# Key tiles of latent and context tokens by 512-column products in one layer of a diffusion backbone

## The chip, the core and the metric

One NeuronCore of a Trainium2 chip runs the whole layer. It has a matrix engine (TensorE, PE in the profile), three engines for elementwise work (VectorE or DVE, ScalarE or ACT, GpSimd or POOL), queues that issue DMA transfers (SyncE's, SP, does most of that), an on-chip memory of 128 partitions (SBUF) and banks in which products accumulate (PSUM, 512 float32 columns a bank and partition). Each engine works through its own queue in order; semaphores hold an instruction back until others are done. The metric is the device time of one execution in microseconds.

## The reference

The layer takes 256 latent tokens `x` and 256 context tokens `ctx`, both 2048 wide, in float32. Cut to what matters here:

```python
h_l = modulate(rms_norm(x, norm1_w), sh1, sc1)          # (1, 256, 2048)
h_c = modulate(rms_norm(ctx, norm1_w), sh1c, sc1c)      # (1, 256, 2048)
gq_l, gk_l, gv_l, gr_l, gaf_l, gab_l, dq_l, dk_l, dv_l = split(h_l @ w_in)
gq_c, gk_c, gv_c, gr_c, gaf_c, gab_c, dq_c, dk_c, dv_c = split(h_c @ w_in)
# gated linear attention, 8 heads of 64/128, forward and backward over chunks of 64 tokens,
#   over the context first, then over the latent tokens
# differential attention, 8 heads: two softmaxes over 512 keys [k_c, k_l], a = p1 - lam * p2
g_a, g_b = split(sigmoid(h_l @ w_gate + b_gate))
x = x + g1 * ((g_a * (gla @ w_proj_gla) + g_b * (diff @ w_proj_diff)) @ w_out)
x = x + g2 * conv_ffn(modulate(rms_norm(x, norm2_w), sh2, sc2))    # width 5632, convolution of 3
```

Only the latent stream is returned. The context needs keys (`gk`, `dk`), values (`gv`, `dv`) and decays, while queries, gates and all that follows are of the latent tokens alone.

## The kernel before

**Products of split halves.** Every float32 operand is split into a high part (rounded to TensorE's fp32r format) and a low part, the difference. A product is then three: high by high, high by low, low by high. ScalarE makes the high half of a weight tile (L211, `whi`), VectorE the low half (L218, `wlo`; in the feed-forward part GpSimd takes some), and the halves of the activations are kept for the whole layer: `A[k]` (tile name `a`) for the latent and `B[k]` (`c`) for the context, for each of 16 K tiles of 128 rows a tile `[128, 2, 256]` with the low half in front and the high half behind it. The lists `H` hold the halves of both.

**Two ways to multiply.** `col_tile` (L243) makes a 128-column piece of a projection of the latent tokens alone, with the output's columns as rows: high weights by both halves of `A[k]` in one product of 512 columns, low weights by the high half, 256 columns. Where latent and context tokens are both wanted, `both_tile` (L334) makes three products of 256 columns for each stream, six a K tile, into the two halves of one bank. `col_tile2` (L760) runs it over 16 K tiles for two key tiles of the GLA heads (`gk`) and seven of the differential heads (`dk`). Values (`gvb`, `dvb`) are made the other way round, activations as the weights and 512 weight columns streaming (`value_rows`, L288).

**The stages.** First the sweep (up to about 132 us): while the modulation weights stream in, each K tile of `x` and `ctx` is normed and modulated (`stage`, L528) and at once multiplied with part of `w_in`: four row groups (`sweep_row`) and three key tiles (`sweep_col`, L562, six products of 256 columns for each), with modulation products (`ab`) for the next K tile between them. Everything in the sweep has a fixed order. Then the GLA stage (to about 450 us), the differential attention with the gate tiles (to about 760), the merge, and the feed-forward part.

**What sets the order.** Outside the sweep a scheduler orders each engine's queue before the run, with a timeline of its own and priorities. In the GLA stage the four head pairs (`gla_pair`, L788) have a high priority, and projections fill in between: `gvb`, `gq`, `gk`, `dk`, `gr`, then the first value chunk `dvb` of the differential heads and the first queries `dq`. A pair is a long serial chain: decay logits `z` on PE, logarithms and scans on ACT and DVE to `rc` (L826), transposed on PE (`kT`, L831), copied, multiplied to `state` (L837), and then scores `sc` (L863) in rounds: first two plain ones, then seven levels of a halving scheme, two levels a round. For a level, POOL makes four differences of the running decay sums (L890 to L893), ACT their exponential (L894), DVE the product with queries and keys (L895), PE the scores, DVE the masked copy (L908). There are two buffers `e` for it, so that a round starts when the scores of the round before have read theirs. At the end come `o` (L914, L917), its sum of squares `oss` (L681) and the norm. The pairs use the same buffers one after another.

The differential stage needs the memory of the GLA stage, so it begins when the fourth pair is done: the first value chunk stands in four accumulator banks until then, and the first query projection `dq` takes one of two banks that `oss` uses as well (`aux_bank`, L1018). In `dv_chunk` (L994) the second chunk takes the K tiles in the order 12 to 15, then 0 to 11, so that context halves of the last tiles come free early: the halves of the keys (`ks`, in `halves`, L1025) are put in their place, later the gates (`C`), one for each `c` tile. Dot products of further modulation weights (`ada_next`, L703: a load into one of two buffers `araw`, and a VectorE product L363) are strewn over all of this, one or half of one for each tile.

Of the kernel before, what the change touches and what calls it, by code (L numbers as in the profile page):

```python
# [9 lines left out]
F32 = mybir.dt.float32  # L10
F32R = mybir.dt.float32r
# [7 lines left out]
P = 128  # L19
D = 2048  # L20
T = 256
KT = D // P
# [129 lines left out]
def layer_kernel(tc, I, out):  # L152
    nc = tc.nc
    V, S, G, PE = nc.vector, nc.scalar, nc.gpsimd, nc.tensor
    es = ExitStack()
    with es:
        cp = es.enter_context(tc.tile_pool(name="const", bufs=1))
        st = es.enter_context(tc.tile_pool(name="stream", bufs=1))
        hp = es.enter_context(tc.tile_pool(name="acts", bufs=1))
# [165 lines left out]

        A, B, C = [], [], []
        (hl, ll), (hc, lc) = H = ([], []), ([], [])
        def spare(k, j, name):  # L330

            return hp.tile([P, 512], F32, tag=f"{'ac'[j]}{k}", name=name)

        def both_tile(b, k, whi, wlo, sl, first, last):  # L334

            for j, (hi, lo) in enumerate(H):
                o = b[:, j * T:(j + 1) * T]
                PE.matmul(o, whi[:, sl], hi[k], start=first and j == 0, stop=False)
                PE.matmul(o, whi[:, sl], lo[k], start=False, stop=False)  # L339
                i = PE.matmul(o, wlo[:, sl], hi[k], start=False, stop=last and j == 1)  # L340
            return i


        cb = cp.tile([P, D], F32, name="cb")
# [25 lines left out]
        with tc.tile_pool(name="first", bufs=1) as p1:  # L370
            kept = tc.keep_in_program_order

            def pinned(*args, **kw):

                return kept(PE.matmul(*args, **kw))  # L375
# [21 lines left out]
            dots_of, at = [], 0  # L397
# [129 lines left out]

            def stage(k, m, streams=(0, 1), lows=()):  # L528

                for s in streams:  # L530
                    Y, n, (hi, lo) = (A, B)[s], "ac"[s], H[s]
                    Y.append(hp.tile([P, 2, T], F32R, tag=f"{n}{k}", name=f"{n}{k}"))
                    hi.append(Y[k][:, 1, :])
                    lo.append(Y[k][:, 0, :])
                for s in streams:
                    x = x_tile(s, k)
                    kept(V.scalar_tensor_tensor(x, x, m[:, 1, s:s + 1], z1[:, s * T:(s + 1) * T],
                                                op0=ALU.mult, op1=ALU.mult))
# [20 lines left out]
                pinned(o, hi[k][:, ts], w[1][:, :n], start=False, stop=False)  # L559
                pinned(o, lo[k][:, ts], w[0][:, :n], start=False, stop=k == KT - 1)  # L560

            def sweep_col(k, w, g, streams=(0, 1)):  # L562
                sl = slice(g * P, (g + 1) * P)
                for s in streams:
                    hi, lo = H[s]
                    o = sweep[4 + g][:, s * T:(s + 1) * T]
                    pinned(o, w[0][:, sl], hi[k], start=k == 0 and s == 0, stop=False)
                    pinned(o, w[1][:, sl], hi[k], start=False, stop=False)
                    pinned(o, w[0][:, sl], lo[k], start=False, stop=k == KT - 1 and s == 1)


            pin[0] = True
# [6 lines left out]
            for s in range(2):  # L579
                o = ss[:, s * T:(s + 1) * T]  # L580
# [401 lines left out]
        with tc.tile_pool(name="diff", bufs=1) as pd:  # L982
# [11 lines left out]
            def dv_chunk(j):  # L994
                banks = [acc_bank("dvb") for _ in range(4)]

                def emptied(t):
                    (V.tensor_copy if t % 2 else S.copy)(dv[:, t, 512 * j:512 * (j + 1)], banks[t])


                turn = [6, 7, 0, 1, 2, 3, 4, 5] if j else list(range(8))
                for q in turn:
                    if q in turn[1:3]:
                        flush((later, latest)[turn.index(q) - 1])
                    raw = fetch(I["w_dv"][j, q].rearrange("p a b -> p (a b)"), 1024)
                    ws = []
                    for a in range(2):
                        def halves_of(a=a):
                            if j or q > 1:
                                ada_next(0.5 if j else 1)  # L1010
                            return split(raw[:, a * 512:(a + 1) * 512], 512)
                        ws.append((2 * q + a, halves_of))
                    value_rows(banks, ws, 512, 2 * turn[0], 2 * turn[-1] + 1, emptied)

            def dq_tile(h):
                ada_next(0.5)
# [8 lines left out]
            def halves(h):  # L1025

                qs[h] = pd.tile([P, 2, T], F32R, tag="qs", bufs=2, name="qs")
                split_act(qs[h][:, 0, :], qs[h][:, 1, :], dq[h])
                ks[h] = [hp.tile([P, 512], F32R, tag=f"c{KT - 4 + 2 * (h % 2) + j}", name="ks") for j in range(2)]
                split_act(*ks[h], dk[h])  # L1030

            pms, pTs = {}, {}
# [49 lines left out]
            def gate_tile(j):  # L1082
                ada_next(GATE_ADA[len(gates)])
                b = acc_bank("gate")
                col_tile(I["w_gate"][j], A, b)
                if j == len(C):
                    C.append(hp.tile([P, 2, T], F32, tag=f"c{j}", name=f"C{j}"))
                gates[j] = C[j % KT][:, j // KT, :]
                S.activation(gates[j], b[:, :T], AF.Identity, bias=vcol("b_gate", j))
                V.tensor_tensor(gates[j], b[:, T:], gates[j], op=ALU.add)  # L1090
# [159 lines left out]
        with tc.tile_pool(name="ffn", bufs=1) as pf:  # L1250
# [65 lines left out]

            def turn(m):

                rows.append([hp.tile([P, 512], F32, tag=f"a{4 * t + m}", name="row") for t in range(2)])
                turned = st.tile([P, 1024], F32, tag="araw", bufs=2, name="turned").rearrange("p (c t) -> p c t", c=4)  # L1320
                for c in range(4):
                    V.transpose(turned[:, c, :], x1[4 * m + c])  # L1322
                for p in range(4):
                    for q in range(8):
                        to = rows[m][q // 4].rearrange("p (c n) -> p c n", c=4)
                        nc.gpsimd.dma_start(to[32 * (q % 4):32 * (q % 4 + 1), :, 32 * p:32 * (p + 1)],  # L1326
                                            turned[32 * p:32 * (p + 1), :, 32 * q:32 * (q + 1)])
# [31 lines left out]
            def done(h, t, n, cols=slice(0, 512)):  # L1359

                o = slice(1024 * h + 512 * n + cols.start, 1024 * h + 512 * n + cols.stop)
                y = hp.tile([P, 512], F32, tag=f"a{8 + (4 * h + 2 * t + n + (cols.start > 0)) % 8}", name="y")[:, :cols.stop - cols.start]
                V.tensor_tensor(y, banks[h][t][n][:, cols], cb[:, o], op=ALU.mult)
                V.tensor_tensor(y, y, rows[2 * h + n][t][:, cols], op=ALU.add)
                nc.scalar.dma_start(out[t * P:(t + 1) * P, o], y)
# [35 lines left out]
```

## Time and profile before

| | |
|---|---|
| median of 3 runs | 1680.33 us (1679.37 to 1680.52) |
| profiled execution | 1679.91 us, its span in the trace 1677.6 us |
| PE busy | 1664.8 us, 10052 products |
| DVE, ACT, POOL busy | 1303.0, 978.6, 340.0 us |
| DMA | 370.82 MB, 221 GB/s over the span |
| first 120 us | DMA at 356 to 408 GB/s, its 16 engines full |

The page's second part cuts the span in 40 slices and shows the busy tenths of each engine; the chain is followed back from the last instruction, at each step to what released it. A row of a timeline gives start, length, engine, line, operation and tiles; lengths of matmuls overlap, so the price of a product is the distance from one start to the next in an unbroken run.

### The profile page before, as it was taken

Reading aid. Unit: us, or ns where it says so; the run is one execution under the profiler, and the core shown is the slowest. Engines: PE = TensorE matmul, PEld = TensorE weight load, DVE = VectorE, ACT = ScalarE, POOL = GpSimd, SP = SyncE. Lnnn points to the kernel's source line nnn. Section 1 sums busy time; section 2 is a strip of 40 time slices with the busy share of each in tenths; the row PEclk is TensorE's granted clock in tenths of the full one; section 3 lists DMA queues with packets and bytes.
Section 4 is the critical chain, followed back from the end, with each engine's and each line's share of the span. In section 5 each row is a group of like instructions: output and inputs, shape, how many; then the busy total and the mean of one; then the engine's idle time right before and its main releaser. Section 6 shows DMA issues by size and latency. Waiting matters only on the chain.

```text
span 1677.6 us, 28522 instructions
## 1 busy us (share of the span) xinstructions
PE 1664.8 (99%) x10052; PEld 1439.8 (86%) x10052; DVE 1303.0 (78%) x2479; ACT 978.6 (58%) x1977; POOL 340.0 (20%) x440
## 2 busy tenths in 40 slices
PE   9999999999999999999999999999999999999998
PEld 7779999998788888888888998888888888888887
DVE  5887877768687988788988897888888787755655
ACT  5335465755356777656766686666666666544443
POOL 0001313232210000001223200222222222684000
PEclk9999999999999999999999999999999999999999
DMA  9996744336564655688887566767777676676664
GB/s 383 408 355 215 227 139 154 126 113 206 171 205 147 187 190 189 205 292 273 272 270 247 178 202 212 237 222 240 239 236 237 223 238 213 211 217 209 216 195 142
DMA packets 110831, 370.82 MB, mean 221 GB/s; under 512 B 14432, under 2 KB 19552, under 8 KB 110688
## 3 DMA queue, kind: packets, MB, share of 16 engines
q1 hardware_dynamic: 102112, 362.51, 64.8%
q10 hardware_dynamic: 4032, 4.37, 0.8%
q0 software_dynamic: 4544, 2.14, 0.6%
q8 instruction: 78, 1.28, 0.3%
q14 instruction: 65, 0.53, 0.1%
HBM read 364.73 MB, written 2.10 MB: 219 GB/s over the span
## 4 chain that ended last, share of the span: by engine, by line
PE 95%; DMA 2%; DVE 2%; ACT 1%; issue 0%; DVEq 0%; SPq 0%; ACTq 0%
PE down L1353 14%; PE upg L269 9%; PE upv L269 9%; PE gate L269 7%; PE upv L271 5%; PE upg L271 5%; PE sweep L375 5%; PE gate L271 4%; PE mix L269 4%; PE mix L271 2%; PE pgb L269 2%; PE pga L269 2%; PE dk L340 2%; PE dvb L286 2%; PE dk L339 2%; PE dvb L285 2%
## 5 line engine op out<-in xcount | busy, mean ns | idle before, releaser
L211 ACT CAST whi<-wraw 128x512 fp32r<-128x512 f32 (+2 forms) x1004 | 605.5, 608 | 392.4 <-DVE wlo L218 111.3
L218 DVE TENSOR_TENSOR wlo<-wraw,whi 128x512 fp32r<-128x512 f32 (+2 forms) x932 | 635.6, 690 | 225.9 <-ACT whi L211 214.0
L269 PE MATMUL upg<-a,whi 128*128 128x512 f32 x656 | 229.0, 391 | 0.0
L269 PE MATMUL upv<-a,whi 128*128 128x512 f32 x656 | 229.0, 391 | 0.0
L1353 PE MATMUL down<-whi,g 128*128 128x512 f32 x704 | 216.6, 389 | 0.0
L271 PE MATMUL upv<-a,wlo 128*128 128x256 f32 x656 | 182.8, 280 | 0.0
L271 PE MATMUL upg<-a,wlo 128*128 128x256 f32 x656 | 182.6, 280 | 0.0
L269 PE MATMUL gate<-a,whi 128*128 128x512 f32 x512 | 179.8, 397 | 0.0
L218 POOL TENSOR_TENSOR wlo<-wraw,whi 128x512 fp32r<-128x512 f32 x72 | 100.5, 1395 | 387.9 <-ACT whi L211 370.7
L363 DVE CUSTOM_DVE_ANT_0 araw<-araw,cb 128x1024 f32<-128x1024 f32 x128 | 162.3, 1270 | 15.5 <-DMA araw<-in_w_ada 15.5
L1353 PEld LDWEIGHTS down<-whi,g 128*128 128x128 f32 x704 | 132.1, 188 | 27.3
L269 PEld LDWEIGHTS upv<-a,whi 128*128 128x128 f32 x656 | 122.4, 187 | 26.6
L269 PEld LDWEIGHTS upg<-a,whi 128*128 128x128 f32 x656 | 122.4, 187 | 26.6
L271 PE MATMUL gate<-a,wlo 128*128 128x256 f32 x512 | 139.9, 283 | 0.0
L1353 PE MATMUL down<-wlo,g 128*128 128x512 f32 x352 | 136.9, 389 | 0.0
L271 PEld LDWEIGHTS upv<-a,wlo 128*128 128x128 f32 x656 | 123.9, 189 | 0.5
L271 PEld LDWEIGHTS upg<-a,wlo 128*128 128x128 f32 x656 | 123.9, 189 | 0.5
L269 PEld LDWEIGHTS gate<-a,whi 128*128 128x128 f32 x512 | 94.3, 188 | 19.6 <-issue 0.7
L271 PEld LDWEIGHTS gate<-a,wlo 128*128 128x128 f32 x512 | 96.4, 188 | 5.7 <-issue 1.8
L269 PE MATMUL mix<-a,whi 128*128 128x512 f32 x256 | 88.8, 396 | 0.0
L1353 PEld LDWEIGHTS down<-wlo,g 128*128 128x128 f32 x352 | 66.1, 188 | 13.8
L1326 POOL DMA_DIRECT2D row<-turned x128 | 69.4, 551 | 26.0 <-DVE turned L1322 17.6
(360 smaller groups left out, 3432.7 us busy)
## 6 DMA issues: line engine op xcount, KB each, us to landing
wraw<-in_w_up SPq DMA_DIRECT2D x164, 512.0 KB, 4.4
araw<-in_w_ada SPq DMA_DIRECT2D x128, 512.0 KB, 5.0
wraw<-in_w_down SPq DMA_DIRECT2D x88, 512.0 KB, 4.3
wraw<-in_w_gate SPq DMA_DIRECT2D x64, 512.0 KB, 4.2
wraw<-in_w_in SPq DMA_DIRECT2D x58, 512.0 KB, 4.3
ada<-in_w_ad SPq DMA_DIRECT2D x52, 512.0 KB, 10.0
wraw<-in_w_proj SPq DMA_DIRECT2D x32, 512.0 KB, 4.7
wraw<-in_w_out SPq DMA_DIRECT2D x32, 512.0 KB, 4.7
```

The source lines that it names most:

```text
L211: copied[0] = S.copy(hi[:, :n], raw)
L218: i = e.tensor_tensor(lo[:, :n], raw, hi[:, :n].bitcast(F32), op=ALU.subtract)
L269: i = PE.matmul(b.rearrange("p (a b) -> p a b", a=2), whi[:, sl], acts[k], start=first, stop=last)
L271: i = PE.matmul(b[:, T:], wlo[:, sl], acts[k][:, 1, :], start=False, stop=last)
L285: PE.matmul(o, lo[k][:, ts], whi[:, sl], start=False, stop=False)
L286: return PE.matmul(o, hi[k][:, ts], wlo[:, sl], start=False, stop=last)
L339: PE.matmul(o, whi[:, sl], lo[k], start=False, stop=False)
L340: i = PE.matmul(o, wlo[:, sl], hi[k], start=False, stop=last and j == 1)
L363: i = V.tensor_tensor_reduce(raw, raw, cb[:, q * 1024:(q + 1) * 1024], 1.0, 0.0, op0=ALU.mult, op1=ALU.add, accum_out=ada2[:, j, q:q + 1])
L375: return kept(PE.matmul(*args, **kw))
L1326: nc.gpsimd.dma_start(to[32 * (q % 4):32 * (q % 4 + 1), :, 32 * p:32 * (p + 1)], turned[32 * p:32 * (p + 1), :, 32 * q:32 * (q + 1)])
L1353: i = PE.matmul(banks[h][t][n], g[:, a, ts], w[n][b], start=k == 0 and (a, b) == (1, 0), stop=k == FT - 1 and b == 1)
```

## The change

The activations of both streams go into one tile a K tile, `X4[k]` of `[128, 4, 256]`: latent low and high, context low and high. `A[k]` is its first half. `both_tile` then takes high and low parts of both streams at once, as an operand of two pieces of 256 columns that lie 512 apart, and makes three products of 512 columns in place of six of 256. `sweep_col` uses the same function.

Since the context halves no longer have tiles of their own, tiles come free only when the latent halves are moved together: in the second value chunk, after each pair of K tiles, a DMA on GpSimd's queue copies the latent halves of the odd K tile into the context's place of the even one, eight moves of 256 KB. The odd tiles are then used for the key halves and the gates, and later work (`spare`, rows, outputs) takes halves of whole tiles by `shared`.

```diff
-        A, B, C = [], [], []
+        X4, A, C = [], [], []
         (hl, ll), (hc, lc) = H = ([], []), ([], [])
+        taken = {}
+        def shared(k, j, name):
+            if (k, name) not in taken:
+                taken[k, name] = hp.tile([P, 1024], F32, tag=f"x{k}", name=name)
+            return taken[k, name][:, j * 512:(j + 1) * 512]
+
         def spare(k, j, name):
-            return hp.tile([P, 512], F32, tag=f"{'ac'[j]}{k}", name=name)
+            return shared(k, j, name)
-        def both_tile(b, k, whi, wlo, sl, first, last):
-            for j, (hi, lo) in enumerate(H):
-                o = b[:, j * T:(j + 1) * T]
-                PE.matmul(o, whi[:, sl], hi[k], start=first and j == 0, stop=False)
-                PE.matmul(o, whi[:, sl], lo[k], start=False, stop=False)
-                i = PE.matmul(o, wlo[:, sl], hi[k], start=False, stop=last and j == 1)
-            return i
+        def both_tile(b, k, whi, wlo, sl, first, last, matmul=PE.matmul):
+            o = b.rearrange("p (a t) -> p a t", a=2)
+            hi, lo = X4[k][:, 1::2, :], X4[k][:, 0::2, :]
+            matmul(o, whi[:, sl], hi, start=first, stop=False)
+            matmul(o, whi[:, sl], lo, start=False, stop=False)
+            return matmul(o, wlo[:, sl], hi, start=False, stop=last)
...
             def stage(k, m, streams=(0, 1), lows=()):
-                for s in streams:
-                    Y, n, (hi, lo) = (A, B)[s], "ac"[s], H[s]
-                    Y.append(hp.tile([P, 2, T], F32R, tag=f"{n}{k}", name=f"{n}{k}"))
-                    hi.append(Y[k][:, 1, :])
-                    lo.append(Y[k][:, 0, :])
+                X4.append(hp.tile([P, 4, T], F32R, tag=f"x{k}", name=f"x{k}"))
+                A.append(X4[k][:, :2, :])
+                for s, (hi, lo) in enumerate(H):
+                    hi.append(X4[k][:, 2 * s + 1, :])
+                    lo.append(X4[k][:, 2 * s, :])
...
-            def sweep_col(k, w, g, streams=(0, 1)):
-                (six products of 256 columns)
+            def sweep_col(k, w, g):
+                both_tile(sweep[4 + g], k, w[0], w[1], slice(g * P, (g + 1) * P), k == 0, k == KT - 1, pinned)
...
                     value_rows(banks, ws, 512, 2 * turn[0], 2 * turn[-1] + 1, emptied)
+                    if j:
+                        nc.gpsimd.dma_start(X4[2 * q][:, 2:, :], A[2 * q + 1])
+                        A[2 * q + 1] = X4[2 * q][:, 2:, :]
...
-                ks[h] = [hp.tile([P, 512], F32R, tag=f"c{KT - 4 + 2 * (h % 2) + j}", name="ks") for j in range(2)]
+                both = hp.tile([P, 1024], F32R, tag=f"x{KT - 3 + 2 * (h % 2)}", name="ks")
+                ks[h] = [both[:, j * 512:(j + 1) * 512] for j in range(2)]
...
-                    C.append(hp.tile([P, 2, T], F32, tag=f"c{j}", name=f"C{j}"))
+                    C.append(shared(2 * (j // 2) + 1, j % 2, "C").rearrange("p (a t) -> p a t", a=2))
```

The scheduler makes a new order of this. Three places, each queue as it stands.

TensorE, the start of a `dk` tile, before: two K tiles, `a` latent and `c` context, `whi` and `wlo` the halves of the weights.

```order
L338 MATMUL dk<-a_288,whi 128x256
L339 MATMUL dk<-a_288,whi 128x256
L340 MATMUL dk<-a_288,wlo 128x256
L338 MATMUL dk<-c_289,whi 128x256
L339 MATMUL dk<-c_289,whi 128x256
L340 MATMUL dk<-c_289,wlo 128x256
L338 MATMUL dk<-a_374,whi 128x256
L339 MATMUL dk<-a_374,whi 128x256
L340 MATMUL dk<-a_374,wlo 128x256
L338 MATMUL dk<-c_375,whi 128x256
L339 MATMUL dk<-c_375,whi 128x256
L340 MATMUL dk<-c_375,wlo 128x256
```

The same two K tiles in the change, `x` being the common tile:

```order
L346 MATMUL dk<-x_280,whi 128x512
L347 MATMUL dk<-x_280,whi 128x512
L348 MATMUL dk<-x_280,wlo 128x512
L346 MATMUL dk<-x_356,whi 128x512
L347 MATMUL dk<-x_356,whi 128x512
L348 MATMUL dk<-x_356,wlo 128x512
```

Twelve products of 256 columns have become six of 512.

TensorE, the last links of the fourth GLA pair before: `sc` are scores (the last round), `o` and `oss` what follows them, `dvb` products of the value chunk, `dq` the first query tile.

```order
L284 MATMUL dvb<-whi,a_1416 128x512
L863 MATMUL sc<-e 128x128 x4
L914 MATMUL o<-qe,state 128x256 x4
L285 MATMUL dvb<-whi,a_1416 128x512
L286 MATMUL dvb<-wlo,a_1416 128x512
L284 MATMUL dvb<-whi,a_1428 128x512
L285 MATMUL dvb<-whi,a_1428 128x512
L286 MATMUL dvb<-wlo,a_1428 128x512
L284 MATMUL dvb<-whi,c_1417 128x512
```

In the change, from the last `dvb` products on:

```order
L284 MATMUL dvb<-whi,x_1279 128x512
L285 MATMUL dvb<-whi,x_1279 128x512
L286 MATMUL dvb<-wlo,x_1279 128x512
L864 MATMUL sc<-e 128x128 x20
L915 MATMUL o<-qe,state 128x256 x4
L918 MATMUL o<-at,gv 128x256 x4
L682 MATMUL oss<-osq,ones 128x256
L682 MATMUL oss<-l,ones 128x256
L269 MATMUL dq<-x_280,whi 128x512
L271 MATMUL dq<-x_280,wlo 128x256
```

Before, `dvb` products stand between all rounds up to `oss`; in the change the last 20 scores (two rounds of two levels and one of one), `o`, `oss` and `dq` follow each other without any. Of the chunk's 192 `dvb` products 19 stood ahead of the pair's `kT` and 173 behind it; in the change 137 stand ahead and 55 behind, 22 of them before `state`.

GpSimd's queue in the change, in the differential stage (`dq` rows are rotations of the third and fourth query tile):

```order
L694 TENSOR_TENSOR rt<-rt,rope 128x256
L1016 DMA x_1120<-x_1195 128x512
L1016 DMA x_1268<-x_1279 128x512
L1016 DMA x_280<-x_356 128x512
L1016 DMA x_431<-x_506 128x512
L1016 DMA x_579<-x_654 128x512
L1016 DMA x_725<-x_744 128x512
L1016 DMA x_849<-x_924 128x512
L1016 DMA x_996<-x_1015 128x512
L695 TENSOR_TENSOR dq<-nraw,rope 128x256
```

Before, the two rotations followed each other; now the eight moves stand between them, those of K tiles 13 and 15 first.

More of the change, by code (lines that the diff above doesn't have):

```diff
@@ L560, in sweep_row @@
                 pinned(o, lo[k][:, ts], w[0][:, :n], start=False, stop=k == KT - 1)
-            def sweep_col(k, w, g, streams=(0, 1)):
[L563 to L569, printed above, removed]
+            def sweep_col(k, w, g):
+                both_tile(sweep[4 + g], k, w[0], w[1], slice(g * P, (g + 1) * P), k == 0, k == KT - 1, pinned)
             pin[0] = True
@@ L1317, in turn @@
             def turn(m):
-                rows.append([hp.tile([P, 512], F32, tag=f"a{4 * t + m}", name="row") for t in range(2)])
+                rows.append([shared(2 * m, t, "row") for t in range(2)])
                 turned = st.tile([P, 1024], F32, tag="araw", bufs=2, name="turned").rearrange("p (c t) -> p c t", c=4)
@@ L1361, in done @@
                 o = slice(1024 * h + 512 * n + cols.start, 1024 * h + 512 * n + cols.stop)
-                y = hp.tile([P, 512], F32, tag=f"a{8 + (4 * h + 2 * t + n + (cols.start > 0)) % 8}", name="y")[:, :cols.stop - cols.start]
+                at = (4 * h + 2 * t + n + (cols.start > 0)) % 8
+                y = shared(8 + 2 * (at // 2), at % 2, "y")[:, :cols.stop - cols.start]
                 V.tensor_tensor(y, banks[h][t][n][:, cols], cb[:, o], op=ALU.mult)
```

## Prediction

> **What bounds the kernel now.** I read the page's busy times and its chain first.
>
> ```profile
> span 1677.6 us, 28522 instructions
> PE 1664.8 (99%) x10052; PEld 1439.8 (86%) x10052; DVE 1303.0 (78%) x2479; ACT 978.6 (58%) x1977; POOL 340.0 (20%) x440
> PE 95%; DMA 2%; DVE 2%; ACT 1%; issue 0%; DVEq 0%; SPq 0%; ACTq 0%
> ```
>
> TensorE is the bound: 95% of the chain that ended last is its matmuls. So what the change takes off PE should count one to one, unless PE then has to wait for something. To see where it waits today I went through the stages in windows of 20 us. Up to 920 us every window after the first two is full to within 0.7 us, with one exception:
>
> ```profile
> 420.00:440.00 20.00, 20.00 (x110) 16.07 (x109) 14.86 (x27) 5.73 (x10) 8.80 (x12) 1.00 0.74 233
> 440.00:460.00 20.00, 16.62 (x92) 13.63 (x91) 11.21 (x29) 8.46 (x21) 0.00 (x0) 1.00 0.35 115
> ```
>
> PE lacks 3.4 us there (second number, busy us of 20). This is the end of the fourth and last gated linear attention (GLA) pair. The chain of waits in that stretch, with start and length:
>
> ```profile
> 397.73 0.44 PE kT L831 x4
> ...
> 403.20 1.02 PE state L837 x16
> 404.23 0.65 PE sc L863 x8
> ...
> 432.74 5.39 DMA araw<-in_w_ada
> 438.26 1.23 DVE araw L363
> ...
> 441.43 0.14 issue
> 441.57 0.71 PE sc L863 x8
> 442.28 0.94 PE o L914 x8
> ...
> 446.39 1.73 PE o L917 x8
> ...
> 451.64 0.34 DVE osq L313
> 452.03 0.50 PE dq L269
> ```
>
> and from the table of waits:
>
> ```profile
> PE dq L269 <- DVE osq L313: 2.1, 1, 2.1
> ```
>
> The pair is a long serial chain over PE, POOL, ACT and DVE (kT, state, six rounds of scores `sc`, `o`, `oss`), and the first query projection `dq` cannot start before it ends, because it needs the PSUM bank that the last `osq` empties. What keeps PE full meanwhile is filler, the value projection `dvb`, whose products stand between the rounds. The prediction turns on how much of it is still there.
>
> **What the new products save.** Pitches (start to start) in unbroken runs of the PE timeline:
>
> ```profile
> 205.27 0.28 PE L338 MATMUL dk<-a,whi 128*128 128x256 f32 x1
> ...
> 206.71 0.28 PE L338 MATMUL dk<-a,whi 128*128 128x256 f32 x1
> ...
> 485.09 0.39 PE L284 MATMUL dvb<-whi,a 128*128 128x512 f32 x1
> ...
> 486.91 0.62 PE L286 MATMUL dvb<-wlo,a 128*128 128x512 f32 x2
> ```
>
> The first two rows are 12 products of 256 columns apart: 1.44/12 = 0.120 us. The last two are 8 products of 512 columns apart: 1.82/8 = 0.2275 us. (The durations 0.28 and 0.39 overlap and are no price.) So two products of 256 become one of 512 for 0.240 - 0.2275 = 0.0125 us less. The mean over the stream is the same amount of work; only a fixed part of about 12 ns per product falls away.
>
> Here a rule of the Trainium skill speaks against the change. "TensorE: Matmul & The Clock Gate", section "Wait — 56ns, not 53.3ns?", gives the fixed cost of a warm matmul as about 2.5 ns beyond its columns; by that a pair saves 2.5 ns and the whole change 1.4 us. The trace does not agree: its 256-column pitch is 120 ns where the page's formula gives 109, so I go by the rows.
>
> - Seven dk and two gk tiles, 16 K tiles each, six products to three: 9 x 16 x 3 = 432 pairs x 0.0125 = **-5.4 us**.
> - The sweep, 9 pairs a K tile: K tiles 0 to 2 wait for loads, so 13 x 9 x 0.0125 = **-1.5 us**. Loads could eat this too:
>
> ```profile
> 102.14 1.75 SPq L347 DMA_DIRECT2D ada<-in_w_ad  x4
> ...
> ada<-in_w_ad SPq DMA_DIRECT2D x23, 512.0 KB, 9.9
> ...
> 115.92 1.86 PE ab L375 x32
> ```
>
> The last modulation weights are issued by 103.9 and take 9.9 us, so they are there at 113.8, used at 115.9: 2.1 us in hand against 1.5 saved. Bounds 0 and -1.8 (all 16 K tiles).
>
> The moving operand is now two pieces of 256 columns, 512 apart. No row shows such an operand. I price it as contiguous (0.2275); the nearest row for the other end is the 256-column pitch twice (0.240), which would leave nothing of the 6.9 us. A price below 0.2275 is excluded, since a piece cannot stream faster than a whole row of columns does.
>
> **What the new order costs.** The scheduler has arranged PE's queue anew. Counted in the order: of the 192 `dvb` products of the first value chunk, 19 stood ahead of the fourth pair's kT and 173 behind it; now 137 stand ahead and 55 behind. Everything else ahead of kT is the same work. So 118 products move ahead of kT: 118 x 0.2275 = **+26.8 us** for kT. Behind it, 22 still stand before `state` (as before), 33 between the scores, and none after the second round: `sc x20`, `o x8`, `oss x2` and `dq` follow each other bare.
>
> In an earlier pair the queue is now also thinner than the chain. In the second pair 16 `gr` products and two `hss` are all that stands between two double rounds: 8 x 0.3475 + 0.45 + the round's own 1.09 = 4.3 us. And from `z` to kT of that pair there are now 20.2 us of PE work. What the chain needs:
>
> ```profile
> 225.50 0.58 PE L801 MATMUL z<-gaT,wa 96*128 96x512 f32 x1
> ...
> 246.26 0.69 DVE L826 TENSOR_TENSOR rc<-rc,qk 128x512 f32<-128x512 f32 x1 [0.66 <-ACT rc L825]
> ...
> 342.17 1.09 PE sc L863 x16
> 342.93 0.46 POOL L890 TENSOR_TENSOR e<-bfb 128x128 f32<-128x128 f32 x1 [1.84 <-PE sc L863]
> 345.56 0.85 POOL L893 TENSOR_TENSOR e<-bfb 128x128 f32<-128x128 f32 x1
> 346.44 0.63 ACT L894 ACTIVATE e<-e 128x512 f32<-128x512 f32 x1 [1.26 <-POOL e L893]
> 347.11 0.69 DVE L895 TENSOR_TENSOR e<-e,qk 128x512 f32<-128x512 f32 x1 [0.96 <-ACT e L894]
> ...
> 276.85 1.09 PE sc L863 x16
> 279.79 0.69 DVE L895 TENSOR_TENSOR e<-e,qk 128x512 f32<-128x512 f32 x1 [0.82 <-ACT e L894]
> ```
>
> A double round: from its scores (342.17) over eight POOL subtractions, ACT's exponential and DVE's product to 347.80, 5.63 us, and 0.14 to PE's next start (the issue row at 441.43): **5.8 us**. A round of one level: 276.85 to 280.48, with the same step **3.8 us**. From `z` to the end of `rc`: 21.5 us. So the second pair waits 5.8 - 4.3 = 1.5 us at the round and up to 1.3 us at kT; I take **+2.0 us** (bounds 0 and 2.8).
>
> Now the end of the fourth pair, walked:
>
> - kT: 397.73 + 26.8 - 5.4 - 1.5 + 2.0 = 419.6. To `state` 5.5 us as before (403.20 - 397.73): 425.1.
> - From `state` to the last `sc` that has filler around it: 1.03 + 0.65, 15 `dvb` (3.4), 0.65, 10 `dvb` (2.3), then the two scores of the first double round, 2 `dvb` apart: their middle at 8.6 us after `state`.
> - Two double rounds, bare: 2 x 5.8 = 11.6. One single round: 3.8.
> - Its scores and the eight `o`: 0.65 + 0.97 + 1.73 = 3.35. From the end of `o` to `dq` 452.03 - 448.12 = 3.9.
> - Sum 8.6 + 11.6 + 3.8 + 3.35 + 3.9 = 31.3. `dq` starts at 425.1 + 31.3 = 456.4, against 452.03: **+4.4 us**.
>
> In these 31 us PE has 33 x 0.2275 = 7.5 us of filler and some 9.6 of its own links (state 1.0, scores 5.4, `o` 2.7, `oss` 0.5), so some 14 us of new idle time swallow the 6.9 saved and more. The old stretch had its own loss (a dot product of the modulation weights that waited for its load, 432.74 to 438.26); in the new order all these dots stand ahead of the second round, so that goes, and the walk has it gone.
>
> **Moving the latent halves.** Eight moves of 256 KB on POOL's queue, after the third query's rope; queued behind them is the fourth's, which waits for the end of the chunk anyway. Nearest rows:
>
> ```profile
> row<-turned POOLq DMA_DIRECT2D x128, 16.0 KB, 3.7
> ...
> rope<-in_rope SPq DMA_DIRECT2D x1, 256.0 KB, 2.7
> ```
>
> About 3.7 us to land. The first move waits for 12 `dvb` products; the first scores that need its freed tile stand 67 products (15 us) in: hidden. The last one starts 3 products before the chunk ends and its K tile is wanted by `dq` 5.7 us later (0.7 + 1.1 of `s` and `hss` + 22 products of a column tile): hidden by 2 us. I cost it at 0; if a move took twice the row, +1.7.
>
> From the gates to the end PE's order is the same. Sum against the profiled execution's own time: 1679.91 + 4.4 = **1684.3 us**. That execution lies 0.42 below the median 1680.33, within the spread of the runs; I add nothing.
>
> **Rivals.** What a measurement of this kernel can tell from no change is about 0.2%, 3.4 us: faster is below 1677.0, slower above 1683.7.
>
> 1. *Not slower: the bare rounds are quick* (0.25). With splits and dots gone from DVE and nothing beside it on POOL, eight subtractions at 0.36 spacing make a double round 0.8 + 2.9 + 0.63 + 0.69 + 0.14 = 5.2 us, the single 3.7, the second pair waits nothing, the sweep gives 1.8: kT 417.3, `dq` 422.8 + 30.0 = 452.8, 1680.7 us. For it: the row 345.56 took 0.85 under load, 0.40 elsewhere. Against: 5.8 is already the quickest double round of the trace; others took 6.3 and more. It decides from 5.4 us a round down.
> 2. *Faster: the old order's waits cover the new ones* (0.10). If the fourth pair reaches `state` as early as before, since POOL, ACT and DVE work run ahead of PE, the saving stays whole: 1679.9 - 6.9 = 1673.0 us. Against: kT stands behind 118 more products in an in-order queue.
> 3. *PE slows down in the gaps* (0.10). Bare double rounds leave PE idle 4.6 us at a time. The run's start:
>
> ```profile
> 1.06 5.16 PE L375 MATMUL sweep<-ones 128*128 128x512 f32 x14 [1.06 <-DVE ones L175]
> 3.78 2.44 PE L375 MATMUL sweep<-ones 128*128 128x512 f32 x8
> ```
>
>    After idling the first six products took 2.72/6 = 0.45 us each, twice the later pitch, though the clock column says 1.00. If that recurs, three rounds, the `o` and the start of `dq` cost some 3 x 0.3 + 1.8 + 1.35, +4: 1688 us. "TensorE: Matmul & The Clock Gate", section "What's actually happening", states that PE's clock halves after an idle window of about 3.4 us; the start agrees, a gap in mid-run is in no row.
> 4. *The moves are late* (0.08): each 256 KB behind POOL's descriptors, `dq` or the fifth head's scores wait: +2 on the forecast, 1686 us.
>
> The forecast has the rest, 0.47, its own range 1681 to 1688. Somewhat over half of it lies beyond 1683.7, rivals 3 and 4 wholly; rival 1 and the rest of it are the same; rival 2 and a trace of rival 1 are faster: slower 0.45, same 0.42, faster 0.13. The range that leaves out most of rival 2 and the far end of rival 3, and takes in most of the dearest price of the split operand (+6.9): 1675 to 1690.
>
> **What would show it.** In the new profile: 512-column dk products at a pitch of 0.2275; the fourth kT some 20 us later, near 419; between it and the first `dq` some 36 us, not 54; the window around 430 to 455 with about 14 us of PE idle, ended by `e` on DVE; `dq` starting near 456; from there on a constant shift against the old trace. The prediction is wrong if that stretch keeps PE full, if the shift at `dq` is negative, or if a new wait appears behind the moves.

## The result, and the profile after

The changed kernel takes **1689.62 us** (median of 6 runs, 1688.71 to 1690.68) against 1680.20 for the kernel before; the ratio is 1.0056, 95% interval 1.0045 to 1.0067. It is slower by 9.4 us. The profiled execution took 1689.73 us.

The page after, its span, busy times and chain:

```profile
span 1687.9 us, 27427 instructions
PE 1663.7 (99%) x9476; PEld 1413.2 (84%) x9476; DVE 1304.4 (77%) x2479; ACT 980.2 (58%) x1977; POOL 342.1 (20%) x448
PE 92%; DMA 4%; DVE 2%; issue 1%; ACT 1%; POOL 1%; SPq 0%; DVEq 0%
```

576 products fewer, and yet TensorE is busy for as long (1663.7 us, 1664.8 before) and on 92% of the chain instead of 95%. Both hints lead to the windows of 20 us. Window, its length, busy us of PE, PEld, DVE, ACT and POOL, then the granted TensorE clock, the DMA share and GB/s:

```profile
280.00:300.00 20.00, 16.27 (x88) 13.17 (x88) 13.75 (x27) 7.75 (x15) 7.13 (x14) 0.91 0.41 130
440.00:460.00 20.00, 10.55 (x62) 8.08 (x60) 8.85 (x18) 5.37 (x13) 5.85 (x14) 0.66 0.10 32
```

Two holes: one of 3.7 us in the second pair, one of 9.5 us at the end of the fourth. And in both the clock column is below 1.00. The table of waits names the same places:

```profile
PE sc L864 <- DVE e L896: 12.8, 4, 4.2
PE dq L269 <- DVE osq L313: 1.5, 1, 1.5
```

Before, that first row read:

```profile
PE sc L863 <- DVE e L895: 1.3, 1, 1.3
```

The TensorE timeline of the fourth pair, with the wait ahead of a row in brackets:

```profile
422.57 0.65 PE L832 MATMUL kT<-ident,rc 128*128 128x128 f32 x4 [0.29 <-DVE rc L827]
...
428.19 1.09 PE L838 MATMUL state<-gv,kn 128*64 128x128 f32 x16
...
442.81 1.78 PE L864 MATMUL sc<-e 64*128 64x128 f32 x16 [2.56 <-DVE e L896]
448.82 2.08 PE L864 MATMUL sc<-e 64*128 64x128 f32 x16 [4.23 <-DVE e L896]
453.14 1.22 PE L864 MATMUL sc<-e 64*128 64x128 f32 x8 [2.24 <-DVE e L896]
454.12 2.08 PE L915 MATMUL o<-qe,state 64*128 64x256 f32 x8
456.13 2.31 PE L918 MATMUL o<-at,gv 128*128 128x256 f32 x8
...
461.13 0.50 PE L269 MATMUL dq<-x,whi 128*128 128x512 f32 x1 [1.51 <-DVE osq L313]
```

This is the bare tail of the forecast: rounds follow each other at 6.0 and 4.3 us with PE waiting in front of each. `dq` starts at 461.1 instead of 452.0. What the forecast had not put into its sum is the lengths: 16 scores take 2.08 us where a round with filler takes 1.09, and the eight `o` from `state` go from 454.12 to 456.13, twice the 0.97 of before. From `dq` on the shift stays: the first `dq` is 9.1 us later than before, the last `down` product (start 1682.38 against 1672.42) 10.0 us.

### The profile page after: what moved, and what is told of

Its sections match the earlier page's. It is cut to its first block, busy times and chain, and to the rows that moved or that the text cites. A ratio compares the mean times of both kernels' runs of the same rounds, so it can differ in the third digit from the quotient of the medians.

```text
span 1687.9 us, 27427 instructions
## 1 busy us (share of the span) xinstructions
PE 1663.7 (99%) x9476; PEld 1413.2 (84%) x9476; DVE 1304.4 (77%) x2479; ACT 980.2 (58%) x1977; POOL 342.1 (20%) x448
## 4 chain that ended last, share of the span: by engine, by line
PE 92%; DMA 4%; DVE 2%; issue 1%; ACT 1%; POOL 1%; SPq 0%; DVEq 0%
PE down L1358 14%; PE upg L269 9%; PE upv L269 9%; PE gate L269 7%; PE upv L271 5%; PE upg L271 5%; PE sweep L382 4%; PE mix L269 4%; PE gate L271 4%; PE mix L271 2%; PE pgb L269 2%; PE pga L269 2%; DMA araw<-in_w_ada 2%; PE dk L346 2%; PE dk L347 2%; PE dk L348 2%
## 5 line engine op out<-in xcount | busy, mean ns | idle before, releaser
L269 PE MATMUL upg<-x,whi 128*128 128x512 f32 x656 | 229.0, 391 | 0.0
L269 PE MATMUL upv<-x,whi 128*128 128x512 f32 x656 | 229.0, 391 | 0.0
L271 PE MATMUL upv<-x,wlo 128*128 128x256 f32 x656 | 182.8, 280 | 0.0
L271 PE MATMUL upg<-x,wlo 128*128 128x256 f32 x656 | 182.6, 280 | 0.0
L269 PE MATMUL gate<-x,whi 128*128 128x512 f32 x512 | 180.0, 397 | 0.0
L269 PEld LDWEIGHTS upv<-x,whi 128*128 128x128 f32 x656 | 122.4, 187 | 26.6
L269 PEld LDWEIGHTS upg<-x,whi 128*128 128x128 f32 x656 | 122.4, 187 | 26.5
L271 PE MATMUL gate<-x,wlo 128*128 128x256 f32 x512 | 139.9, 283 | 0.0
L271 PEld LDWEIGHTS upv<-x,wlo 128*128 128x128 f32 x656 | 123.9, 189 | 0.5
L271 PEld LDWEIGHTS upg<-x,wlo 128*128 128x128 f32 x656 | 123.9, 189 | 0.5
```

The lines of the kernel that those rows point to most:

```text
L269: i = PE.matmul(b.rearrange("p (a b) -> p a b", a=2), whi[:, sl], acts[k], start=first, stop=last)
L271: i = PE.matmul(b[:, T:], wlo[:, sl], acts[k][:, 1, :], start=False, stop=last)
```

## The experiments

Times are medians in us, next to the median of the kernel before in the same comparison; the ratio has its 95% interval.

| run | TensorE order | products | this | before | ratio |
|---|---|---|---|---|---|
| the change | new | 512 | 1689.62 | 1680.20 | 1.0056 (1.0045 to 1.0067) |
| e1 | old, by K tiles | 512 | 1677.18 | 1680.71 | 0.9979 (0.9970 to 0.9988) |
| e2 | new, by K tiles | 256, old tiles | 1696.89 | 1680.71 | 1.0098 (1.0084 to 1.0112) |
| e3 | old, by K tiles | 256, common tiles | 1683.43 | 1680.71 | 1.0015 (1.0007 to 1.0024) |
| e4 | new, dummies behind scores | 512 | 1688.97 | 1680.71 | 1.0046 (1.0033 to 1.0060) |
| e5 | old, all queues, by K tiles | 512 | 1677.17 | 1680.18 | 0.9982 (0.9974 to 0.9991) |
| e6 | old, all queues, by K tiles | 256, common tiles | 1682.19 | 1680.18 | 1.0016 (1.0007 to 1.0025) |
| e8 | old, exact | 512 | 1673.06 | 1680.34 | 0.9958 (0.9946 to 0.9971) |
| e9 | old, exact | 256, common tiles | 1680.20 | 1680.34 | 0.9997 (0.9988 to 1.0006) |
| e10 | old, exact, one dot later | 512 | 1673.24 | 1680.34 | 0.9958 (0.9946 to 0.9971) |
| e11 | new, dummies ahead of scores | 512 | 1684.78 | 1680.97 | 1.0024 (1.0014 to 1.0034) |
| e12 | old, fourth pair's end new | 512 | 1685.31 | 1680.97 | 1.0029 (1.0017 to 1.0040) |

e7 is a probe of its own. Every run computes the whole layer.

**Separating products from order (e1, e2, e3).** A table holds the sequence in which one kernel's TensorE products stand after the sweep, up to the first gate tile; at the end of the program each product of the other kernel is tied behind its predecessor in it (an edge of order alone, no wait). An entry a.n of the table stands for n products from the a-th of the program on. Where one kernel has three products and the other six, the K tile was put down whole at the place of its first product.

```diff
+ORDER = ("0.25 32.2 25.7 36.5 50.2 34.1 41.3 53.2 35.1 44.3 56.2 52.1 55.1 58.1 62.2 65.2 68.2 64.1 67.1 70.1 74.2 77.2 "
...
+            row = []
+            for r in ORDER.split():
+                a, n = map(int, r.split("."))
+                for u in units[a:a + n]:
+                    row += u
+            for x, y in zip(row, row[1:]):
+                tc.add_manual_dep(y, x.name, mybir.DependencyInfo(mybir.DependencyClass.NoSync, mybir.DependencyReason.DATA),
+                                  reason="order")
```

> The changed kernel, but TensorE's queue from the sweep to the first gate tile stands in the order of the kernel before (a K tile's three products where its six stood). Theory A (the products save what was priced, the new order alone costs): 1680.2 - 6.9 = 1673.3 us, no window with more than 4 us of TensorE idle between 280 and 460. Theory B (common tiles and moves cost, whatever the order): 1680 to 1685 us. If the saving is covered by old waits: 1680.

> The kernel before, but TensorE's queue from the sweep to the first gate tile stands in the order of the changed kernel (six products where the three stand). Theory A: the order costs what the result lacks, 9.4 + 6.9 = 16.3 us: about 1696.5, with gaps at the second pair's third double round and in the fourth pair's last rounds, as in the changed kernel. Theory B: near 1680 to 1685, because the order is not what costs.

For e3, the common tiles and moves stay and `both_tile` makes six products again:

```diff
-            o = b.rearrange("p (a t) -> p a t", a=2)
-            hi, lo = X4[k][:, 1::2, :], X4[k][:, 0::2, :]
-            matmul(o, whi[:, sl], hi, start=first, stop=False)
...
+            for j, (hi, lo) in enumerate(H):
+                o = b[:, j * T:(j + 1) * T]
+                matmul(o, whi[:, sl], hi[k], start=first and j == 0, stop=False)
...
```

> Common tiles and moves of the latent halves, but six products of 256 columns and TensorE's order of the kernel before. Moves hidden, as priced: 1680.2, within 0.2%. If a move is late for dq or the fifth head (rival 4) or the tiles coming free later matter: 1682 to 1685.

Measured: e2 is 16.2 us slower than before, as theory A had it (16.3): the order costs, with the old products as with the new. But e1 gained 3.5 instead of 6.9, and e3 lost 2.7 where nothing was expected. The products were worth 6.3 between e3 and e1; some 3 us seemed to lie in the tiles or the moves. Theory A was half in doubt.

**Where the 3 us were (e5, e6, e8, e9).** In e1 to e3 the other queues were left to the scheduler; VectorE's differed from the old order in some 45 places. e5 and e6 tie them too.

```diff
+        for engine, order in (("DVE", ORDER_DVE), ("Activation", ORDER_ACT), ("Pool", ORDER_POOL)):
+            in_order([i for i in ins[:cut[0]] if str(i.engine).endswith(engine)], order)
```

> As the run with the new products in TensorE's old order, but VectorE, ScalarE and GpSimd too have the order of the kernel before, instruction by instruction, as far as the end of the GLA stage's program (there they differed in 45, 33 and some 70 places by a few positions). If those small shifts cost the 3.9 us that the first run lacks (one gk product waits 2.0 us for VectorE's wlo): 1680.7 - 6.9 = 1673.8 us. If the common tiles or the moves cost: still near 1677.

> Common tiles, moves and six products of 256 columns, all four queues in the order of the kernel before to the end of the GLA stage. If the moves and the tiles are hidden and the 2.7 us of the third run came from the small shifts on VectorE's queue: 1680.7, within 0.2%. If the tiles or the moves themselves cost: 1683.4.

No change: 1677.17 and 1682.19. So the small shifts were not it. But in e5 and e6, as in e1 and e3, one row of the waits has no counterpart in the kernel before. From e6's TensorE timeline:

```profile
240.79 0.28 PE L542 MATMUL gk<-x,whi 128*128 128x256 f32 x1
242.78 0.39 PE L543 MATMUL gk<-x,wlo 128*128 128x256 f32 x1 [1.71 <-DVE wlo L411]
```

In the kernel before `dk` products stand at this time. The scheduler had split the first K tile of that `gk` tile: two products with the high weights early, the other four 46 products later, when the low weights are there. Putting the K tile down whole at its first product's place brought the low-weight product forward into a wait. The 3 us were of my own making. e8 and e9 keep every product's own place (TensorE's table ends at the first gate tile here too); a merged product stands where the later of its two stood:

```diff
-                for u in units[a:a + n]:
-                    row += u
+                row += mine[a:a + n]
```

> New products, all four queues in the order of the kernel before to the end of the GLA stage, and now product by product: where a K tile's six products stood apart, its three do too. In the earlier runs with the old order each K tile was put down whole at the place of its first product, and in all of them one gk product waited 1.7 to 2.0 us for its low weights (wlo) near 240 us. If that wait was made by my placing, and the tiles and moves are free: 1680.2 - 6.9 = 1673.3 us, no wait of gk. If the common tiles or the moves cost: still 1676 to 1677.

> Common tiles, moves and six products, each queue in the exact order of the kernel before (TensorE's to the end of the program). If tiles and moves are hidden: as before, 1680.2, within 0.2%. If they cost what the earlier runs seemed to say: 1682 to 1683.

Both as the theory said: 1673.06 (1673.3 expected) and 1680.20 (1680.2). **The tiles and the eight moves cost nothing. The products of 512 columns are worth 1680.20 - 1673.06 = 7.1 us. The new order costs 1689.62 - 1673.06 = 16.6 us.** The intervals leave the products some room: e8's alone allows 4.9 to 9.1 us below the kernel before. In e8's windows the hole is small and the clock full:

```profile
440.00:460.00 20.00, 17.88 (x98) 14.96 (x96) 14.74 (x35) 13.18 (x32) 1.61 (x2) 1.00 0.36 104
```

**How much of it is the fourth pair (e12).** The stretch from the fourth kT to the first `dq` is put in as the changed kernel has it, the rest of TensorE's order stays old. Only TensorE's queue is tied here; the other three are left to the scheduler, as in e1. In the table 1498 and what follows are value products, 978.4 is kT:

```diff
-1484.1 978.4 1485.1
+1484.2
...
-1498.3
+1498.99 978.4 1597.22
...
```

> The new products in the exact old order, except that the fourth pair's stretch from kT to the first dq stands as in the changed kernel: 118 dvb products move ahead of kT, 55 stay behind it. Theory: this alone, not the rest of the new order, makes the fourth pair bare: kT at 390.8 + 26.8 = 417.6, dq 5.5 + 32.9 later at 456.0 (454.4 if the half clock costs nothing there), against 444.9: 1673.1 + 11.1 = 1684.2 us. The other 5.4 us to 1689.6 then belong to the second pair (a wait of 3.7, slow products 1.7). If the fourth pair alone is not what costs: below 1680.

1685.31: 12.3 us above e8 (11.1 expected). The waits are the changed kernel's to the digit (2.56, 4.23 and 2.24 us ahead of the three rounds), and the window shows the same half-empty stretch:

```profile
440.00:460.00 20.00, 11.38 (x66) 8.93 (x65) 9.44 (x23) 6.35 (x16) 4.93 (x12) 0.68 0.05 19
```

So moving 118 value products ahead of one instruction, kT, explains 12.3 of the 16.6 us, the slow products behind the gaps included. That e12 leaves three queues free and e8 ties them is a difference between the two; in the old order it made none (1677.18 in e1, 1677.17 in e5), in this one it was not tried. The other 4.3 (1689.62 - 1685.31) are a remainder. In the two traces 3.3 of it stand at the first `dq` (461.13 against 457.87), and the second pair is the only other place up to there where the changed kernel's TensorE stood for long.

**What the clock is worth (e4, e11, e7).** Dummy products fill part of the gaps, so that TensorE works but nothing moves.

```diff
+FILL = {(1, 2): 20, (3, 0): 12, (3, 2): 20, (3, 4): 12}
...
+                    for _ in range(warm):
+                        i = PE.matmul(bs[0][:, T:], hl[0][:, :P], hl[0], start=True, stop=True)
...
```

> The changed kernel in its own order, with dummy products of 256 columns (into an unused half of a score bank, 20, 12, 20 and 12 of them) standing where TensorE is idle: after the second pair's second double round and after the fourth pair's first three double rounds. No work is taken away. If TensorE's clock drops in the gaps (rival 3): the products behind a gap go at the usual pitch (16 score products 1.09 us, not 2.08), some 1.7 us in the second pair and 3.3 in the fourth come back: 1689.6 - 5.0 = 1684.6 us, clock 1.00 at 280 to 300 and over 0.9 at 440 to 460. If the slow rows have another cause, such as late semaphores of the scores: 1689.6, unchanged.

1688.97, 0.65 us less: on its face, the clock is worth nothing. The trace says why not to believe it. The dummies wrote into the other half of the bank that holds a round's scores, and stood behind them; VectorE's masked copy of the scores waited for them, with the next round's `e` behind it:

```profile
454.23 0.44 DVE L938 COPY_PREDICATED at<-masks,sc 128x256 f32<-128x256 uint8 x1 [2.07 <-PE sc L894]
```

(The order was put down by K tiles here too, and a `dk` product of the second pair had a wait of 2.0 us that the changed kernel has not.) e11 puts the same dummies ahead of the scores, and every queue has the changed kernel's exact order:

```diff
+FILL = {(1, 4): 20, (3, 2): 12, (3, 4): 20, (3, 6): 12}
...
+                    for _ in range(warm):
+                        i = PE.matmul(bs[0][:, T:], hl[0][:, :P], hl[0], start=True, stop=True)
...
                     for c in range(2):
                         cq = 1 - c if off else c
```

> The changed kernel with all its queues in its own order, dummy products (20, 12, 20, 12 of 256 columns) again, but put ahead of a round's scores instead of behind them, because behind them VectorE's masked copy waited 2.07 us for them in the first try (same tile). What the half clock costs in the changed kernel, by its rows: in the second pair 1.0 us on 16 scores and 0.7 on the first dk products, in the fourth 0.9 and 0.5 on scores and 1.25 on o and oss. If that is all on the path: 1689.6 - 4.3 = 1685.3 us. If the first try showed the whole worth of it: 1689.

1684.78 (1685.3 expected), 4.8 us less: **the half clock costs some 4 to 5 us** of the changed kernel's time. In the traces 3.9 of it stand at the first `dq` (461.13 against 457.27), most of the rest arises near 775 us, at full clock. Nor did all of the clock come back in e11's profiled execution: the scores of one double round of the fourth pair still took 2.08 us (last row below). The second pair's scores after the wait, and the `dk` products behind them, go at full speed again (in the changed kernel 2.08 us for the scores, and 0.35 to 0.6 between the starts of the first `dk` products):

```profile
286.49 1.16 PE L1063 MATMUL sc<-e 64*128 64x128 f32 x16 [1.28 <-DVE e L1095]
287.58 0.50 PE L538 MATMUL dk<-x,whi 128*128 128x512 f32 x1
287.92 0.39 PE L539 MATMUL dk<-x,whi 128*128 128x512 f32 x1
288.15 0.40 PE L540 MATMUL dk<-x,wlo 128*128 128x512 f32 x1
...
446.72 2.08 PE L1063 MATMUL sc<-e 64*128 64x128 f32 x16 [1.86 <-DVE e L1095]
```

Last, a probe by itself behind the kernel before:

```diff
+        for gap, block in [(0, 60)] + [(g, 40) for g in (1, 2, 3, 4, 5, 6, 8, 12)] + [(3, 8)] * 4 + [(3, 40)]:
...
+            for _ in range(gap):
+                keep(V.tensor_tensor(x, x, x, op=ALU.max))
...
+            for _ in range(block):
+                keep(PE.matmul(b[:, :T], w[:, :P], w[:, T:], start=True, stop=True))
```

> The kernel before with a probe behind its last product: blocks of 40 products of 256 columns, between them waits of 1, 2, 3, 4, 5, 6, 8 and 12 VectorE operations of 128x512 (0.69 us each, and about 1 us of copies), then four blocks of 8 with waits of 3 and one of 40. If the clock drops after an idle time of about 3.4 us (rival 3): full pitch 0.12 after the waits of 1 to 3, half speed (0.22 to 0.24) for the first products after those of 4 and more, longest after 12. If idle time does nothing: 0.12 everywhere and only the first product of a block late.

The expectation was wrong: no block ran at full pitch throughout. After the shortest wait between two blocks, 1.97 us, the 40 products took from 1685.40 to 1691.78, the start of the next product: 6.4 us, where the pitch of 0.12 gives 4.8. What decides is shown in the last section.

**A try to go on (e10).** In VectorE's table 608.1 is the dot product of modulation weights that waits for its load at 438 us.

```diff
-476.6 601.5 608.1 482.5
+476.6 601.5 482.5
...
-489.1 492.1 491.1
+489.1 492.1 608.1 491.1
```

> As the run with the new products in the exact old order, but one dot product of modulation weights on VectorE, which in the kernel before waits 2.8 us for its load in front of the fourth pair's third double round, stands behind the fourth pair's last osq. The wait of 1.26 us of TensorE ahead of the score products goes: 1672.0 us against 1673.3. If the round is bound by GpSimd and ScalarE instead: no change against that run.

1673.24 against 1673.06: no difference in the medians, although TensorE's waits for `e` ahead of scores fell from 1.1 us in e8's trace to 0.2, and the first `dq` starts at 443.84 instead of 444.95. Why the medians do not follow is not shown. e8 stays the best version: the change with the old order beats both kernels, 0.42% below the one before (0.29 to 0.54).

## Why the prediction came true, and where its steps were off

The forecast was 1684.3, slower at 0.45; measured 1689.6, slower, inside 1675 to 1690 by 0.4. The direction and the mechanism are shown (e2, e12). The size was short by 5.3, and most of that is one thing, TensorE's clock behind the gaps. That the result lies inside the range is in part luck: it is above the forecast's own 1681 to 1688 and above rival 3's 1688, and the upper end of 1690 was set by a dear price of the split operand, which did not come.

- **What the products save, -6.9.** Shown: 7.1 by e9 and e8. The split operand streams as a contiguous one. In the new trace, the first and the last of 14 `dk` products in a row:

```profile
199.76 0.39 PE L347 MATMUL dk<-x,whi 128*128 128x512 f32 x1
...
202.71 0.39 PE L348 MATMUL dk<-x,wlo 128*128 128x512 f32 x1
```

  2.95/13 = 0.227 us. 7.1 us over 576 pairs (432 and the sweep's 144) is 12.4 ns a pair. The Trainium skill ("TensorE: Matmul & The Clock Gate", section "Wait — 56ns, not 53.3ns?") has a fixed cost of about 2.5 ns; an estimate from it makes 1.4 us of the whole. The measurement decides: the fixed part of these products is some five times that, and 1.4 us lies outside e8's interval too.
- **The sweep, -1.5.** The first `z` starts at 154.3 instead of 155.8. Right. Loads took little of it: `ab` products now wait 0.4 us in all for their weights, a row that the kernel before does not have.
- **The second pair, +2.0 (0 to 2.8).** Too small. PE waited 3.73 us at one double round, and none at kT. The round took 8.35 us (scores at 277.93 and 286.28), not 5.8. The chain of waits shows what the price from a quiet round left out:

```profile
278.00 0.69 PE sc L864 x8
278.76 1.49 POOL e L891
280.26 0.86 POOL e L892
281.12 0.36 POOL e L893
281.48 0.37 POOL e L894
281.88 0.64 ACT e L895
283.39 0.26 DVE wlo L218
284.20 0.74 DVE nraw L321
284.94 0.60 DVE wlo L218
285.54 0.61 DVE e L896
```

  The first subtraction took 1.49 us where the quiet rounds had 0.46, and on VectorE a norm and two splits of weights stood between the two `e` products. The forecast took the quickest double round of the trace for a place where three engines are shared.
- **kT at 419.6, state 5.5 later.** 422.6 and 5.6. The 3.0 us too much come mainly from the second pair: its extra wait of 1.7, and products at half clock behind it (in e11, where they go at full clock, kT starts at 420.88, 1.7 earlier).
- **31.3 us from state to dq.** 32.9. The walk's links of 5.8 and 3.8 us measured 6.0 and 4.3, the scores and `o` 5.1 (453.14 to 458.28) instead of 3.35, from the end of `o` to `dq` 2.85 instead of 3.9. With the gaps mostly kept warm (e11) the stretch from `state` to `dq` is 30.9 us (426.4 to 457.3). The forecast's "none after the second round" is not quite the order: six more `dvb` stand behind the first double round; the sum does not use them.
- **The moves, 0.** Right (e9). They land in 2.9 us, less than the 3.7 of the forecast. One sign of being wrong did appear, a new wait behind the moves, but on ScalarE, where it costs nothing:

```profile
x<-x POOLq DMA_DIRECT2D x8, 256.0 KB, 2.9
...
ACT ks L236 <- DMA x<-x: 6.2, 2, 4.3
```

- **Rival 1** (bare rounds quick) falls: 6.0 us a round, not 5.2. **Rival 2** falls with e12. **Rival 4** falls with e9. **Rival 3, the clock, happened** beside the forecast, priced at +4, measured at 4 to 5. It was given a chance of 0.10 as an alternative; it belonged into the sum. With most of its effect gone (e11) the walk comes out within a microsecond: `dq` at 457.3, 456.4 forecast, and 1684.78 us, 1684.3 forecast. Some of this closeness is luck, since the second pair's wait was 1.7 us too small and the end of `o` to `dq` 1.05 too long. The step that failed is the sentence against it, that a gap in mid-run is in no row. The run's start was a row for it, and the walk had found gaps of 4.6 us. The Trainium skill ("TensorE: Matmul & The Clock Gate", section "What's actually happening") has the half clock after an idle window of about 3.4 us; these traces agree, and show it after windows that are partly busy too (last section).

What stays open: the shift grows from 9.1 us at the first `dq` to 10.0 at the end. Of that 0.9, 0.7 arises in the first `pga` products (the merge) near 775 us, where one waits 0.42 us for its low weights; the traces of e8, e11 and e12 have no such wait, and whether every execution of the changed kernel has it is not shown. And the 4.3 us left for the second pair are a remainder: no run puts the new order into that pair alone, and the dummies stood in both pairs at once.

## What to carry to other kernels

A change of products and tiles can make a scheduler order everything anew, and here its new order cost more than twice what the products gained: when a scheduler sets the order, time the change with the old order tied as well (product by product, not in larger pieces), and keep whichever wins. Filler products were worth more behind the start of the serial chain than ahead of it: standing ahead, they made the chain start later by their whole length and left its waits without cover. And a gap on TensorE can cost more than its length, since what follows it may run at half speed.

## What the runs showed of the hardware

**TensorE's clock follows windows of 3.41 us, and a window need not be empty to halve the next one.** The records of the granted clock change on a grid of 3.41 us. The changed kernel's second pair, and its fourth, cut on that grid (second number PE's busy us, third column from the right the clock):

```profile
282.74:286.15 3.41, 0.00 (x0) 0.00 (x0) 3.41 (x6) 3.14 (x7) 0.99 (x2) 1.00 0.40 111
286.15:289.56 3.41, 3.28 (x19) 2.89 (x20) 3.41 (x10) 0.41 (x1) 1.96 (x4) 0.50 0.52 161
289.56:292.97 3.41, 3.41 (x16) 2.81 (x16) 2.61 (x5) 1.91 (x4) 1.44 (x3) 1.00 0.30 112
436.34:439.76 3.42, 3.42 (x25) 2.35 (x24) 1.65 (x5) 0.76 (x2) 2.30 (x7) 1.00 0.82 275
439.76:443.17 3.41, 0.85 (x9) 0.44 (x9) 2.90 (x4) 1.59 (x3) 1.15 (x2) 1.00 0.24 68
443.17:446.58 3.41, 1.42 (x15) 1.13 (x12) 2.02 (x5) 0.63 (x1) 2.76 (x8) 0.50 0.43 142
...
453.41:456.82 3.41, 3.41 (x18) 2.67 (x18) 0.77 (x2) 0.00 (x0) 0.00 (x0) 0.50 0.00 0
456.82:460.24 3.42, 2.76 (x12) 1.77 (x10) 0.25 (x1) 2.37 (x8) 0.00 (x0) 1.00 0.00 0
```

The empty window halves the clock of the next one, and a full one brings the clock back. But the window that was busy for 0.85 of 3.41 us halves the next one too. In the probe:

```profile
1682.18:1685.59 3.41, 1.44 (x11) 1.13 (x10) 1.81 (x3) 0.00 (x0) 0.00 (x0) 1.00 0.00 0
1685.59:1689.00 3.41, 3.41 (x17) 3.41 (x17) 0.00 (x0) 0.00 (x0) 0.00 (x0) 0.50 0.00 0
1689.00:1692.42 3.42, 3.17 (x26) 2.86 (x24) 0.21 (x1) 0.00 (x0) 0.00 (x0) 1.00 0.00 0
...
1794.82:1798.24 3.42, 2.47 (x9) 2.00 (x9) 0.73 (x3) 0.00 (x0) 0.00 (x0) 0.50 0.00 0
1798.24:1801.65 3.41, 0.00 (x0) 0.00 (x0) 3.19 (x5) 0.00 (x0) 0.00 (x0) 0.50 0.00 0
```

A busy share of 42% (1.44 of 3.41) was enough to lose the clock; so a wait of 2 us could do it. Short blocks with waits of 3.5 us between them never got it back, and the fourth pair stayed at half speed for four windows, 13.65 us. The Trainium skill ("TensorE: Matmul & The Clock Gate", section "What's actually happening") gives the window and speaks of an idle one; in these rows a window less than half busy does the same. The border is not sharp: one window of the kernel before, busy for 1.47 us, was followed by full clock (rows below). With all traces cut on their grids, every window at full clock after the first 20 us that was busy for up to 1.44 us was followed by half clock, four of eight between 1.46 and 1.58 us were, and none from 1.70 us on. The way back takes more: half-speed windows busy for up to 2.47 us stayed at half speed, those busy for 3.04 us or more were followed by full clock. The ends of matmuls in a trace are modelled, which may blur both borders.

```profile
448.44:451.85 3.41, 1.47 (x7) 0.92 (x5) 2.48 (x5) 3.10 (x9) 0.00 (x0) 1.00 0.22 54
451.85:455.26 3.41, 3.23 (x18) 2.81 (x19) 3.27 (x12) 1.59 (x3) 0.00 (x0) 1.00 0.25 100
```
